# The down projection of three quarters by seven products, for two panels at a time

## The chip, the cores and the metric

The kernel runs on one core of a Trainium2 chip. The metric is the device time of one execution in microseconds, the median of several runs; lower is better.

## The reference, cut to what matters

One step of one layer of a hybrid decoder for 512 prompt tokens and 8 sample tokens, which share all weights. Attention and gated linear attention give `mix`; the change lies in what follows it:

```
def merge_and_ffn(x, ..., w_o, g_norm2, w_up, w_down):
    ...
    h = x + mix @ w_o
    f = jnp.square(jax.nn.relu(rmsnorm(h, g_norm2) @ w_up))      # w_up (1024, 4096)
    return h + f @ w_down                                        # w_down (4096, 1024)
y_prompt, y_sample = rmsnorm(xp, g_final), rmsnorm(xs, g_final)
```

## The kernel before, in words

**Layout.** Activations lie transposed: 128 rows of the model dimension on the partitions, 8 tiles of them (k), 520 columns (512 prompt tokens and 8 sample tokens). `HC` is half of the columns, 260; `halves` shows a tile as two such halves. D = 1024, KT = 8.

**Precision.** Each matrix product is made of three products of fp32r numbers: high part by high part, high by low, low by high (`passes`). A weight is loaded as a panel (128 output columns, 8 k-tiles, 512 KB) by SP's queue, and split in pieces of 4 k-tiles (512 wide): ScalarE copies the high part (`whi`, L128), VectorE subtracts it from the panel for the low part (`wlo`, L131). Activations are split likewise: `hh`, `hl` for the normalized residual H, `fh`, `fl` for the squared relu.

**Direct panels.** `panel_mm` makes one panel with 2 halves x 8 k x 3 = 48 products of 260 columns (L301).

**Pairs by seven products.** `pair_mm` (L229) makes two panels at once with the Strassen-Winograd scheme: the rows of the activations are halved (k 0 to 3, and 4 to 7), the columns too, and of the two panels' weights. Seven products P1 to P7 of 4 k x 3 = 84 matmuls replace 96. They need sums of weights and of activations. Activation sums: `Th`, `Tl` (high and low parts) hold for each k of the first half the four sums of the two rows k and k + 4 and the two column halves; `column_sums` makes them on VectorE as H is made. Weight sums: the loaded panel `sums` is completed by an accumulating DMA on POOL's queue (`load_sums`, L115, up to 28 us ahead); two VectorE adds make two more (`pair_sums`, tile `s`, 512 wide each). P1, P6, P7, P4 accumulate one behind the other in the PSUM bank x, P5 and P3 in e, P2 in a, where P1's result was copied. The order on TensorE is P1, P5, P6, P3, P7, P2, P4. What is done with a result comes as `then(name, a, e, x)` after that product, and "T0", "T1" at the start of the next pair. `lead(i + 1, ...)` splits the next panel's pieces on the way (0: `pair_sums`; 1: P1's piece; 2: P6's with P3's, 1024 wide, and P5's; 3: P7's).

**The order of work.** In the feed-forward part ScalarE and VectorE run strictly in the order of the program: `act`, `add` and `stt` (L128, L131, L134) pass each instruction to `turn`, which chains it behind the last one of its engine. TensorE is chained too (`behind`). `pace` issues copies of the caches (DRAM to DRAM, on POOL's queue).

**Stages.** W_o makes H panel by panel. Then four quarters (qd) of 1024 columns of w_up: 8 panels as four pairs (`up_pair`), each squared relu split into fh, fl, then 8 down panels of w_down's rows for this quarter, added up in `dd`. Up pairs take neighbouring panels i and i + 1. In quarters 0 to 2 the 8 down panels are direct; quarter 0 copies to dd and squares H for the norm into `acc`; quarter 1 spreads the column sum with a matmul by ones (`spread`, rv = 1 / (mean square + eps)); quarter 2 multiplies dd by rv and adds H. In quarter 3 rv is applied to f, and the down panels are made in a last loop (L1500) in column parts of 280 and 240, with the final norm and the output behind them. In an up pair of quarters 0 to 2, f is the first panel's tile and t the second's; the names `P` of the tiles in the trace are PSUM results of P5 and P6 that ScalarE keeps in SBUF (the `keep` in `up_pair`).

## Time and profile before

| | |
|---|---|
| median of 3 runs | 890.13 us (889.88 to 890.97) |
| profiled execution | 890.22 us |
| its span, first to last instruction | 888.3 us |
| mean granted clock of TensorE | 0.997 |
| TensorE busy | 876.6 us, 7962 matmuls |
| VectorE busy | 605.0 us, 1187 instructions |
| ScalarE busy | 428.0 us, 874 instructions |
| memory | 153.31 MB read, 54.17 MB written |

The span is what the trace covers; the execution's own time is 1.9 us longer. Busy times are sums over the instructions of an engine; engines work beside each other. Rows of the timeline read: start in us from the span's start, duration, engine, line, operation, out<-in, shape, and in brackets the idle time ahead of it with the engine that ended it. The products of a panel or pair are a row of matmuls without a gap where the next one is always ready.

### The profile page before, as it was taken

The numbers are of one execution on the slowest core, as the hardware profiler recorded it, in microseconds if no ns is written. First come the engines' busy times: TensorE is split into PE (matmuls) and PEld (weight loads), VectorE is DVE, ScalarE is ACT, GpSimd is POOL, SyncE is SP. The second block draws the span as 40 slices with busy tenths as digits, with TensorE's granted clock in tenths as the row PEclk, the third lists the DMA queues.
The fourth block names the chain that finished last, engine by engine and source line by source line (L and its number), as shares of the span: only waits on it lengthen the run. The fifth ranks groups of instructions, "written<-read, shape, count | busy, mean of one in ns | idle before, by whom it ended". The sixth has DMA issues, their size and how long they took to land.

```text
span 888.3 us, 19424 instructions
## 1 busy us (share of the span) xinstructions
PE 876.6 (99%) x7962; PEld 859.1 (97%) x7962; DVE 605.0 (68%) x1187; ACT 428.0 (48%) x874; POOL 92.6 (10%) x143
## 2 busy tenths in 40 slices
PE   9999999999999999999999999999999999999996
PEld 9999999999999999999999999999999999999995
DVE  6877566775957949695755778636864585579843
ACT  7233424452635536454633557623752375248732
POOL 1110000001111302101000200011101110110000
PEclk9999999999999999999999999999999999999998
DMA  7476465324445443125798875579748775974302
GB/s 258 134 262 215 130 214 200 110 74 149 159 163 186 158 160 140 57 97 191 251 365 296 301 217 167 190 217 281 232 172 261 240 235 184 282 241 148 143 24 74
DMA packets 44385, 168.29 MB, mean 189 GB/s; under 512 B 5821, under 2 KB 10949, under 8 KB 42473
## 3 DMA queue, kind: packets, MB, share of 16 engines
q1 hardware_dynamic: 34552, 98.98, 32.1%
q0 software_dynamic: 9456, 67.59, 23.7%
q8 instruction: 62, 1.02, 0.4%
q10 hardware_dynamic: 288, 0.49, 0.2%
q14 instruction: 27, 0.21, 0.1%
HBM read 153.31 MB, written 54.17 MB: 234 GB/s over the span
## 4 chain that ended last, share of the span: by engine, by line
PE 97%; DVE 1%; DMA 1%; ACT 0%; issue 0%; SPq 0%; DVEq 0%; ACTq 0%
PE mps L301 64%; PE mps L229 17%; PE mps L1500 5%; PE lev L896 1%; PE mps L467 1%; PE sps L642 1%; PE pvp L675 1%; PE gpo L1005 1%; PE gpu L1009 1%; PE ptp L659 1%; PE vps L606 1%; PE gpo L1007 1%; DMA xr<-in_xT 1%; PE gso L1077 0%; PE gop L1029 0%; PE gsp L1094 0%
## 5 line engine op out<-in xcount | busy, mean ns | idle before, releaser
L128 ACT ACTIVATE whi<-raw 128x512 fp32r<-128x512 f32 (+1 forms) x234 | 143.7, 621 | 260.9 <-PE mps L301 225.4
L301 PE MATMUL mps<-uh,whi 128*128 128x260 f32 x896 | 255.8, 286 | 0.0
L301 PE MATMUL mps<-ul,whi 128*128 128x260 f32 x896 | 255.7, 285 | 0.0
L301 PE MATMUL mps<-uh,wlo 128*128 128x260 f32 x896 | 255.2, 285 | 0.0
L131 DVE TENSOR_TENSOR wlo<-raw,whi 128x512 fp32r<-128x512 f32 (+1 forms) x234 | 156.2, 678 | 45.6 <-ACT whi L128 43.3
L301 PEld LDWEIGHTS mps<-uh,wlo 128*128 128x128 f32 x896 | 168.7, 188 | 2.1 <-issue 1.5
L301 PEld LDWEIGHTS mps<-ul,whi 128*128 128x128 f32 x896 | 168.6, 188 | 1.2 <-issue 0.3
L301 PEld LDWEIGHTS mps<-uh,whi 128*128 128x128 f32 x896 | 168.7, 188 | 1.1 <-issue 0.7
L301 PE MATMUL mps<-fh,wlo 128*128 128x260 f32 x384 | 108.5, 283 | 0.0
L301 PE MATMUL mps<-fh,whi 128*128 128x260 f32 x384 | 108.4, 282 | 0.0
L301 PE MATMUL mps<-fl,whi 128*128 128x260 f32 x384 | 108.1, 282 | 0.0
L229 PE MATMUL mps<-Th,whi 128*128 128x260 f32 x256 | 72.5, 283 | 0.4 <-DVE t L131 0.4
L229 PE MATMUL mps<-Tl,whi 128*128 128x260 f32 x256 | 72.3, 282 | 0.1
L301 PEld LDWEIGHTS mps<-fh,whi 128*128 128x128 f32 x384 | 72.3, 188 | 0.0
L301 PEld LDWEIGHTS mps<-fh,wlo 128*128 128x128 f32 x384 | 72.2, 188 | 0.0
L229 PE MATMUL mps<-Th,wlo 128*128 128x260 f32 x256 | 72.2, 282 | 0.0
L301 PEld LDWEIGHTS mps<-fl,whi 128*128 128x128 f32 x384 | 72.2, 188 | 0.0
L229 PE MATMUL mps<-hl,whi 128*128 128x260 f32 x192 | 54.2, 282 | 0.0
L229 PE MATMUL mps<-hh,wlo 128*128 128x260 f32 x192 | 54.2, 282 | 0.0
L229 PE MATMUL mps<-hh,whi 128*128 128x260 f32 x192 | 54.1, 282 | 0.0
L229 PEld LDWEIGHTS mps<-Th,whi 128*128 128x128 f32 x256 | 48.2, 188 | 0.6 <-DVE t L131 0.6
L229 PEld LDWEIGHTS mps<-Tl,whi 128*128 128x128 f32 x256 | 48.1, 188 | 0.3 <-DVE Tl L131 0.3
(370 smaller groups left out, 1838.2 us busy)
## 6 DMA issues: line engine op xcount, KB each, us to landing
raw<-in_w_in SPq DMA_DIRECT2D x55, 512.0 KB, 4.4
raw<-in_w_down SPq DMA_DIRECT2D x32, 512.0 KB, 4.1
sums<-in_w_up SPq DMA_DIRECT2D x16, 512.0 KB, 4.2
sums<-in_w_up POOLq DMA_DIRECT2D x16, 512.0 KB, 8.0
raw<-in_w_up SPq DMA_DIRECT2D x16, 512.0 KB, 5.8
sx<-in_state SPq DMA_DIRECT2D x8, 512.0 KB, 4.4
sx<-dV SPq DMA_DIRECT2D x8, 512.0 KB, 4.8
out_sgla<-sx POOLq DMA_DIRECT2D x8, 512.0 KB, 5.0
```

Of the source, the lines that this page charges most:

```text
L128: return self.turn("ACT", self.nc.scalar.activation(*args, **kw))
L131: return self.turn("DVE", self.nc.vector.tensor_tensor(out, a, b, op=op))
L229: mm = nc.tensor.matmul(o, w[:, k], u, start=(n in ("P1", "P5") and k == 0 and y == 0), stop=(k == 3 and y == 2), skip_group_check=True)
L301: mm = self.nc.tensor.matmul(o[:, :HC], wt, x[:, k, j * HC:(j + 1) * HC], start=(k == 0 and n == 0), stop=(k == kt - 1 and n == 2))
L467: self.last = nc.tensor.matmul(ps[i][:, j, :HC], wt, u[:, k, j * HC:(j + 1) * HC], start=(k == 0 and n == 0), stop=(k == KT - 1 and n == 1))
L606: nc.tensor.transpose(pt[:, r * P:(r + 1) * P], vt[:, r * P:(r + 1) * P], self.c["ident"])
L642: m = nc.tensor.matmul(pss[hh][:, hp, c], Q[rows, i, b * P:(b + 1) * P], K[rows, i, ks], start=True, stop=True)
L659: nc.tensor.transpose(pt[:, hh, x], prs[hp][:, hh, x * P:(x + 1) * P], self.c["ident"])
L675: m = nc.tensor.matmul(po[64 * hh:64 * hh + 64, hp * P:(hp + 1) * P], v, pTs[hp][:, hh, x], start=(x == first), stop=(x == 1))
L896: m = self.nc.tensor.matmul(out, w, x, start=True, stop=True)
L1005: nc.tensor.matmul(po[:, :256], ST[:, c], V[:, c], start=True, stop=(c == 0))
L1500: nc.tensor.matmul(ps, w, u[:, kk, cc], start=(kk == 0 and x == 0), stop=(kk == KT - 1 and x == 2))
```

## The change

It makes the down projection of quarters 0 to 2 in pairs of panels, through `pair_mm` as the up projection is. For that:

- An up pair is now made of panels i and i + 4 of the quarter, so that it gives the rows k and k + 4 of f together, of which `sums`, `high` and `low` in `up_pair` make the four column sums of squared tiles. Sum 0 is written where the second half of hh, hl for the first four k was (that half is no longer written), sums 1 and 2 in a new tile `FT`, sum 3 in the second half of fh, fl for the first four k. The square of f moves from VectorE to ScalarE. The last up pair of a quarter (`end`) has an order of its own.
- `down_pair` adds each product's result to dd (`put`) when it is there: P5's, P6's, P7's, P3's, P2's and P4's. In quarter 0 the first put to each part of dd is a copy on ScalarE.
- `extras`: H is written to the DRAM tile `Hd` in the W_o stage (POOL's queue); quarter 0 loads it back to square it (SP's queue), quarter 2 adds it to dd by an accumulating DMA (POOL's queue). The reciprocal of quarter 1 is made in four parts of 130 columns.
- In `pair_mm` P7's piece of a pair behind a direct panel, and the weight sums of the next pair, are made after P5; a hook "T2" stands there too. The last loop takes k in the order 0, 1, 2, 4, 5, 6, 3, 7, and cache copies that were issued ahead of it are issued within it.

The diff, cut:

```diff
 def pair_mm(self, acts, then):
-        if not first and self.panels[i - 1][1] != PAIR:
-            self.pair_piece(i, "P7")
         if before:
             before("T0")
...
             if n == "P1":
                 if before:
                     before("T1")
-                if first:
+            elif n == "P5":
+                if before:
+                    before("T2")
+                if "P7" not in self.ready[i]:
                     self.pair_piece(i, "P7")
-                elif pair:
-                    self.lead(i + 1, 0)
-            elif n == "P5":
                 self.pair_piece(i, "P4" if first else "P2")
-                if first:
+                if pair:
                     self.lead(i + 1, 0)
...
-            if n == "P2" and pair:
+            if n == "P2" and pair and not then(n + " ends"):
                 self.lead(i + 1, 3)

 def up_pair(self, p, work, k, fh, fl, T, copies, rv):
-        end, short = k == KT - 2, rv is not None and k == KT - 2
+        end, short = k == 3, k == 3 and rv is not None
+        def sums(*steps):
+            f, t = v["f"], v["t"]
+            if "c" not in v:
+                v["c"] = p.tile([P, 3, HC], F32, tag="tr", name="tr", bufs=2)
+            c = v["c"]
+            for n in steps:
+                if n == 1:
+                    self.add(c[:, 0], t[:, two], f[:, two], op=ALU.subtract)
+                elif n == 0:
+                    self.add(f[:, two], f[:, one], f[:, two], op=ALU.subtract)
+                elif n == 2:
+                    self.stt(c[:, 1], c[:, 0], -1.0, f[:, one], op0=ALU.mult, op1=ALU.subtract)
+                else:
+                    self.stt(c[:, 2], c[:, 1], -1.0, t[:, one], op0=ALU.mult, op1=ALU.subtract)
+        def place(n):
+            return (v["f"][:, two], v["c"][:, 0:2], v["c"][:, 2])[n], *T(n, k)
+        def high(n):
+            c, hi, lo = place(n)
+            self.act(hi, c, AF.Copy)
+        def low(n):
+            c, hi, lo = place(n)
+            self.add(lo, c, hi.bitcast(F32), op=ALU.subtract)
...
             elif n == "P7":
-                v["t"] = work()
-                self.add(v["t"][:, two], x, v["P5"])
+                f, t = v["f"], v["t"] = work(), work()
+                self.add(t[:, two], x, v["P5"])
...
+                self.add(f[:, two], e, v["P6"])
+            elif n == "P7 later":
+                f, t = v["f"], v["t"]
+                if not short:
+                    self.act(t[:, two], t[:, two], AF.Relu, scale=-1.0)
+                self.act(f[:, two], f[:, two], AF.Relu)
+                if T and end:
+                    self.act(t[:, two], t[:, two], AF.Square)
+            elif n == "P2":
+                f = v["f"]
+                self.act(f[:, one], a, AF.Relu)
+                self.act(f, f, AF.Square)
...
+                if T and end:
+                    split(0, f, one)
+                    sums(1, 0)
...
             elif n == "T0":
+                f, t = v["f"], v["t"]
+                self.act(t[:, one], x, AF.Relu, scale=-1.0)
+                if T and end:
+                    high(0)
+                    self.act(t[:, one], t[:, one], AF.Square)
+                    low(0)
+                    sums(2, 3)
+                elif T:
                     self.act(t, t, AF.Square)
+                    split(0, f, one)
+                    sums(1, 0, 2, 3)
...
+            elif n == "T1":
+                if T and end:
+                    high(1)
+                    low(1)
+                    self.act(fh[:, k + 4], v["t"], AF.Copy)
+                else:
+                    split(4, v["t"])
+                    if T:
+                        high(0)
+            elif n == "T2" and T:
+                if end:
+                    high(2)
+                    self.add(fl[:, k + 4], v["t"], fh[:, k + 4].bitcast(F32), op=ALU.subtract)
+                    low(2)
+                else:
+                    high(1)
+                    high(2)
+                    for n in range(3):
+                        low(n)
+
+def down_pair(self, k, dd, qd, also):
+        def put(x, cc, o, sign=1):
+            d = dd[:, k + x, cc]
+            if qd == 0 and (x, cc) not in put.begun:
+                put.begun.add((x, cc))
+                self.act(d, o, AF.Copy, scale=float(sign))
+            elif sign < 0:
+                self.add(d, d, o, op=ALU.subtract)
+            else:
+                self.add(d, o, d)
+        put.begun = set()
+        def then(n, a=None, e=None, x=None):
+            if n == "P1":
+                self.act(a, x, AF.Copy)
+            elif n == "P5":
+                put(1, two, e, -1)
+            elif n == "P6":
+                put(0, two, x)
+            elif n == "P7":
+                put(1, two, x, -1)
+                put(0, two, e)
+            elif n == "P2":
+                put(0, one, a)
+            elif n == "P4":
+                self.pace(1)
+            elif n == "T0":
+                put(1, one, x, -1)
+            also(n)
+        return then

 def run(self):
         for qd in range(4):
-            order += [(I["w_up"][qd * 8 + i:qd * 8 + i + 2], PAIR) for i in range(0, 8, 2)]
-            order += [(I["w_down"][i][:, qd * 8:qd * 8 + 8], KT) for i in range(8)]
+            order += [(I["w_up"][qd * 8 + i:qd * 8 + i + 5:4], PAIR) for i in range(4)]
+            ks = slice(qd * 8, qd * 8 + 8)
+            if qd < 3:
+                order += [(I["w_down"][i:i + 2, :, ks], PAIR) for i in range(0, 8, 2)]
+            else:
+                order += [(I["w_down"][i][:, ks], KT) for i in range(8)]
...
+                nc.gpsimd.dma_start(Hd[:, k], H[:, k])
...
+            def T(n, k):
+                return ((hh[:, k, HC:], hl[:, k, HC:]), (FT[:, k, 0:2], FT[:, k, 2:4]), (fh[:, k, HC:], fl[:, k, HC:]))[n]
+            def extras(qd, k):
+                v = {}
+                def also(n):
+                    if qd == 0:
+                        if n == "P1":
+                            for x in range(2):
+                                v[x] = acc if k + x == 0 else work()
+                                self.load(v[x], Hd[:, k + x])
+                        elif n == "P4":
+                            for x in range(2):
+                                self.act(v[x], v[x], AF.Square)
+                                if k + x:
+                                    self.add(acc, acc, v[x])
+                    elif qd == 1:
+                        if n == "P1" and k == 0:
...
+                            self.turn("DVE", nc.vector.tensor_scalar(halves(rv), pr[:, :, :HC], 1 / D, EPS,
+                                                                     op0=ALU.mult, op1=ALU.add))
+                        elif n == "P4":
+                            c = slice(65 * k, 65 * k + 130)
+                            self.turn("DVE", nc.vector.reciprocal(rv[:, c], rv[:, c]))
+                    elif n in ("P4", "T0"):
+                        x = k + (n == "T0")
+                        self.add(dd[:, x], dd[:, x], rv, op=ALU.mult)
+                        nc.gpsimd.dma_start(dd[:, x], Hd[:, x], accum_op=ALU.add)
+                return also
...
-                for k in range(KT):
-                    ps = self.panel_mm(fh, fl)
-                    dv = halves(dd[:, k])
-                    if qd == 0:
-                        self.turn("DVE", nc.vector.tensor_copy(dv, ps))
-                        sq = work() if k else acc
-                        self.act(sq, H[:, k], AF.Square)
-                        if k:
-                            self.add(acc, acc, sq)
-                    else:
-                        self.add(dv, ps, dv)
-                    if qd == 2:
-                        self.add(dd[:, k], dd[:, k], rv, op=ALU.mult)
-                        self.add(dd[:, k], dd[:, k], H[:, k])
-                    if qd == 1 and k == 0:
-                        spread()
-                    self.pace(k % 2)
-            self.pace(1000)
+                for k in range(0, KT, 2):
+                    self.pair_mm(down_acts, self.down_pair(k, dd, qd, extras(qd, k)))
...
-                    for kk in range(KT):
+                    for kk in (0, 1, 2, 4, 5, 6, 3, 7):
...
+                    if j == 0 and k > 2:
+                        self.pace(1 if k < KT - 2 else 1000)

```

VectorE in a middle up pair of the third quarter (qd 2), from its first add on a result in PSUM (`t<-mps,P`): before, where the first row adds P3's result (f) and the third P7's (t), and the weight pieces are the next pair's,

```order
L131 TENSOR_TENSOR t<-mps,P_9369 128x260
L131 TENSOR_TENSOR wlo<-raw,whi 128x512
L131 TENSOR_TENSOR t<-mps,P_9351 128x260
L131 TENSOR_TENSOR wlo<-s,whi 128x1024
L131 TENSOR_TENSOR wlo<-sums,whi 128x512
L134 SCALAR_TENSOR_TENSOR t<-t 128x520
L131 TENSOR_TENSOR wlo<-sums,whi 128x512
L131 TENSOR_TENSOR fl<-t,fh 128x520 x2
L131 TENSOR_TENSOR s<-sums,raw 128x512
L131 TENSOR_TENSOR s<-s,raw 128x512
L131 TENSOR_TENSOR wlo<-raw,whi 128x512
L131 TENSOR_TENSOR wlo<-rb,whi 128x512
```

and now, where both adds wait for P7 and stand in the first two rows (t, then f), `tr`, `FT` and `hl` belong to the column sums, and the last low part is that of sum 3:

```order
L131 TENSOR_TENSOR t<-mps,P_9532 128x260
L131 TENSOR_TENSOR t<-mps,P_9558 128x260
L131 TENSOR_TENSOR wlo<-s,whi 128x1024
L131 TENSOR_TENSOR wlo<-sums,whi 128x512 x2
L131 TENSOR_TENSOR fl<-t,fh 128x260
L131 TENSOR_TENSOR tr<-t 128x260
L131 TENSOR_TENSOR t<-t 128x260
L134 SCALAR_TENSOR_TENSOR tr<-tr,t 128x260 x2
L131 TENSOR_TENSOR fl<-t,fh 128x520
L131 TENSOR_TENSOR hl<-t,hh 128x260
L131 TENSOR_TENSOR FT<-tr,FT 128x520
L131 TENSOR_TENSOR fl<-tr,fh 128x260
```

A 520-wide square (`t<-t`, L134) is gone; four column sums (`tr<-tr,t` twice, `tr<-t`, `t<-t`) and three low parts have come, and `s` stands further on, behind them.

ScalarE at the same place, from the high part of P5's piece: before, where the relu of t's second half, the relu of f's first half, P7's weight copy, and the relu and square of t follow it,

```order
L128 ACTIVATE whi<-sums 128x512
L128 ACTIVATE t<-t 128x260
L128 ACTIVATE t<-mps 128x260
L128 ACTIVATE whi<-sums 128x512
L128 ACTIVATE t<-mps 128x260
L128 ACTIVATE t<-t 128x520
L128 ACTIVATE fh<-t 128x520
L128 ACTIVATE mps<-mps 128x260
L128 ACTIVATE fh<-t 128x520
```

and now:

```order
L128 ACTIVATE whi<-sums 128x512
L128 ACTIVATE t<-t 128x260 x2
L128 ACTIVATE t<-mps 128x260
L128 ACTIVATE t<-t 128x520
L128 ACTIVATE whi<-sums 128x512
L128 ACTIVATE t<-mps 128x260
L128 ACTIVATE t<-t 128x520
L128 ACTIVATE fh<-t 128x260
L128 ACTIVATE mps<-mps 128x260
L128 ACTIVATE fh<-t 128x520
L128 ACTIVATE hh<-t 128x260
```

The relu of f's second half and the square of f (520 wide) now stand on ScalarE between the relu of t and the weight copy for P7's piece; the copies of the column sums begin at the end.

VectorE at the start of the third quarter's down stage, where the low parts of the last squared tile are made: before, with the panel's add, rv and H for each panel,

```order
L131 TENSOR_TENSOR wlo<-raw,whi 128x512
L134 SCALAR_TENSOR_TENSOR t<-t 128x520
L131 TENSOR_TENSOR fl<-t,fh 128x520 x2
L131 TENSOR_TENSOR wlo<-raw,whi 128x512 x2
L131 TENSOR_TENSOR dd<-mps,dd 128x520
L131 TENSOR_TENSOR dd<-dd,rv 128x520
L131 TENSOR_TENSOR dd<-dd,H 128x520
L131 TENSOR_TENSOR wlo<-raw,whi 128x512 x2
L131 TENSOR_TENSOR dd<-mps,dd 128x520
L131 TENSOR_TENSOR dd<-dd,rv 128x520
L131 TENSOR_TENSOR dd<-dd,H 128x520
```

and now:

```order
L134 SCALAR_TENSOR_TENSOR tr<-tr,t 128x260 x2
L131 TENSOR_TENSOR FT<-tr,FT 128x520
L131 TENSOR_TENSOR dd<-dd,mps 128x260
L131 TENSOR_TENSOR fl<-t,fh 128x520
L131 TENSOR_TENSOR fl<-tr,fh 128x260
L131 TENSOR_TENSOR wlo<-sums,whi 128x512
L131 TENSOR_TENSOR wlo<-raw,whi 128x512
L131 TENSOR_TENSOR s<-sums,raw 128x512
L131 TENSOR_TENSOR s<-s,raw 128x512
L131 TENSOR_TENSOR dd<-mps,dd 128x260
L131 TENSOR_TENSOR wlo<-rb,whi 128x512
L131 TENSOR_TENSOR wlo<-raw,whi 128x512
L131 TENSOR_TENSOR dd<-dd,mps 128x260
```

Of the puts, `dd<-dd,mps` on the third row is P5's, `dd<-mps,dd` P6's, which stands behind two low parts of weights and the two sums `s`.

96 lines of the change are left out of this document (42 added, 54 removed).

## Prediction

> **What bounds the kernel now.** I read the page's busy shares and its chain first, then busy time by stage, then the order in time of VectorE and ScalarE inside one pair.
>
> ```profile
> span 888.3 us, 19424 instructions
> PE 876.6 (99%) x7962; PEld 859.1 (97%) x7962; DVE 605.0 (68%) x1187; ACT 428.0 (48%) x874; POOL 92.6 (10%) x143
> PE 97%; DVE 1%; DMA 1%; ACT 0%; issue 0%; SPq 0%; DVEq 0%; ACTq 0%
> ...
> 655.50:701.40 45.90, 45.90 (x386) 45.90 (x385) 22.16 (x32) 13.41 (x24) 5.77 (x7) 1.00 0.81 264
> 701.50:741.60 40.10, 40.10 (x338) 40.10 (x338) 30.57 (x49) 26.78 (x54) 3.30 (x5) 1.00 0.59 198
> ...
> L301 PE MATMUL mps<-fh,wlo 128*128 128x260 f32 x384 | 108.5, 283 | 0.0
> ```
>
> TensorE (PE) is busy 99% and holds 97% of the chain. The two window rows are the direct down stage of one quarter and the up stage of the next (after the length: PE, weight load, DVE, ACT, POOL busy, clock, DMA share, GB/s). TensorE has no gap in either. VectorE (DVE) is busy 22.2 of 45.9 us in the down stage, but 30.6 of 40.1 in the up stage by pairs, and the change puts work into both. The last row: 24 down panels hold 384 products of each of three kinds, 16 x 3 = 48 a panel.
>
> **The saving.** A panel's end shows when VectorE reads it:
>
> ```profile
> 686.22 0.70 DVE L131 TENSOR_TENSOR dd<-mps,dd 128x520 f32<-128x520 f32 x1 [3.84 <-PE mps L301]
> 691.96 0.70 DVE L131 TENSOR_TENSOR dd<-mps,dd 128x520 f32<-128x520 f32 x1 [3.84 <-PE mps L301]
> ...
> 706.31 0.39 ACT L128 ACTIVATE P<-mps 128x260 f32<-128x260 f32 x1 [1.07 <-PE mps L229]
> 716.35 0.39 ACT L128 ACTIVATE P<-mps 128x260 f32<-128x260 f32 x1 [0.46 <-PE mps L229]
> ```
>
> 5.74 us a panel is 0.1196 us a product; a pair (7 x 4 x 3 = 84 products) takes 10.04. Two panels cost 11.48, so each of the 12 new pairs saves 12 products or 1.44 us: **17.2 us**, if TensorE stays fed. The Trainium skill, "TensorE: Matmul & The Clock Gate", section "Wait — 56ns, not 53.3ns?", gives a warm product its column count over 2.4 GHz plus about 2.5 ns. As an estimate from that page 260 columns take 0.111 us and the saving is 16.0; the trace differs with its 0.1196, and the trace decides.
>
> **What the up pairs pay.** In an up pair of quarters 0 to 2 VectorE gains the four differences of column sums and the low parts of three tiles, and loses one 520-wide square, which goes to ScalarE (ACT). The prices are distances from start to start in one run of each engine:
>
> ```profile
> 710.61 0.43 DVE L131 TENSOR_TENSOR t<-mps,P 128x260 f32<-128x260 f32 x1 [0.30 <-PE mps L229]
> 710.96 1.22 DVE L131 TENSOR_TENSOR wlo<-s,whi 128x1024 fp32r<-128x1024 f32 x1
> 712.09 0.68 DVE L131 TENSOR_TENSOR wlo<-sums,whi 128x512 fp32r<-128x512 f32 x1
> 712.69 0.69 DVE L134 SCALAR_TENSOR_TENSOR t<-t 128x520 f32<-128x520 f32 x1
> 713.30 0.68 DVE L131 TENSOR_TENSOR wlo<-sums,whi 128x512 fp32r<-128x512 f32 x1
> 715.09 1.53 DVE L131 TENSOR_TENSOR fl<-t,fh 128x520 fp32r<-128x520 f32 x2 [1.11 <-ACT fh L128]
> 716.54 0.68 DVE L131 TENSOR_TENSOR s<-sums,raw 128x512 f32<-128x512 f32 x1
> 717.26 0.69 DVE L131 TENSOR_TENSOR s<-s,raw 128x512 f32<-128x512 f32 x1
> 717.87 0.69 DVE L131 TENSOR_TENSOR wlo<-raw,whi 128x512 fp32r<-128x512 f32 x1
> ...
> 831.70 0.43 DVE L134 SCALAR_TENSOR_TENSOR t<-mps,rv 128x260 f32<-128x260 f32 x1 [0.93 <-PE mps L229]
> 832.16 0.43 DVE L134 SCALAR_TENSOR_TENSOR t<-mps,t 128x260 f32<-128x260 f32 x1
> ...
> 711.07 0.42 ACT L128 ACTIVATE t<-t 128x260 f32<-128x260 f32 x1
> 712.05 0.39 ACT L128 ACTIVATE t<-mps 128x260 f32<-128x260 f32 x1 [0.56 <-PE mps L229]
> 713.47 0.39 ACT L128 ACTIVATE t<-mps 128x260 f32<-128x260 f32 x1 [0.51 <-PE mps L229]
> 713.89 0.64 ACT L128 ACTIVATE t<-t 128x520 f32<-128x520 f32 x1
> 714.44 0.62 ACT L128 ACTIVATE fh<-t 128x520 fp32r<-128x520 f32 x1
> 714.96 0.37 ACT L128 ACTIVATE mps<-mps 128x260 f32<-128x260 f32 x1
> 715.27 0.62 ACT L128 ACTIVATE fh<-t 128x520 fp32r<-128x520 f32 x1
> ...
> 711.85 0.28 PE L229 MATMUL mps<-Th,whi 128*128 128x260 f32 x1
> 538.74 0.39 PE L229 MATMUL mps<-Th,whi 128*128 128x260 f32 x1 [0.39 <-DVE t L131]
> 538.97 0.28 PE L229 MATMUL mps<-Tl,whi 128*128 128x260 f32 x1
> ```
>
> VectorE steps: 260 wide 0.35, 512 0.60, 520 0.61, 1024 1.13; 0.46 (260) or 0.72 (512) if the next reads what it wrote. ScalarE: 260 wide 0.31, 512 0.52, 520 0.55, and 0.42 from a relu to the square that reads it. From a ScalarE end to the VectorE read 0.03 (714.44 + 0.62 to 715.09); from the next product's start to the read of the last one 0.20 (711.85 to 712.05).
>
> Follow a middle up pair from X, its first low part (fl, 260). VectorE's list up to the second PSUM add f is six steps of 0.35, two of 0.46, two 520 (1.22), three 512 (1.80), and the two sums s (0.72 + 0.60): f starts at X + 7.37. Then ScalarE: relu of f's half when f is done (+0.46), next relu +0.31, square +0.42, P7's weight copy +0.55, T0's relu +0.52, square +0.42, high copy +0.55, its own 0.42 and 0.03: the next X is f + 3.68. One round is 11.05 us against TensorE's 10.04. VectorE itself has only about 10.0 us of work in it; it waits some 1.0 us for that ScalarE chain. So each middle pair comes **1.0 us** later than TensorE needs. At first this is covered by weights split ahead.
>
> Quarter's first pair is on time (VectorE has slack behind a down pair): its chain starts when P2 can be read, 7.17 + 1.44 + 0.20 = 8.81, and X of the second pair is 2.91 later, 11.72, or 1.68 into that pair. X is then 2.69 and 3.70 into the third and fourth, and f of the fourth at F = 11.07.
>
> **What the first down pair pays.** Its product P7 accumulates on the bank that P6 left, so it waits until P6's result is added to dd. In quarters 1 and 2 that add stands on VectorE behind low parts and two weight sums. From F: two relus, square, relu, square of f (0.11, 0.46, 0.77, 1.08, 1.50), high copy at 2.17, fl 2.62, two sums 2.97 and 3.43, high copy of T0 3.89, its low part 4.34, sums 4.69 and 5.15, copy of FT, then VectorE without a gap: FT 5.80, P5's put 6.41, fl 6.76 and 7.37, P7 7.72, P2 8.32, s 8.92 and 9.64, P6's put 10.25. It lasts 0.43; TensorE restarts 0.06 behind (538.26 + 0.42, the add of the row below, to 538.74) and loses 0.11 on its first product (0.23 instead of 0.12): 10.85. P7 starts at 11.07 + 10.85 = 21.9, on time would be 10.04 + 5.74 = 15.8: **6.1 us** in quarter 2, earlier waits of TensorE included. In quarter 1 the rv step adds 0.3 and the ones products, part of the time now, take off 0.7: **5.7**.
>
> ```profile
> 538.26 0.42 DVE L131 TENSOR_TENSOR t<-mps,P 128x260 f32<-128x260 f32 x1
> 649.27 1.04 PE L1442 MATMUL r<-acc,ones 128*128 128x260 f32 x4
> 649.96 0.47 PE L229 MATMUL mps<-Th,whi 128*128 128x260 f32 x1
> ...
> 538.47 0.61 ACT L128 ACTIVATE whi<-sums 128x512 fp32r<-128x512 f32 x1
> 540.47 0.39 ACT L128 ACTIVATE t<-mps 128x260 f32<-128x260 f32 x1 [0.29 <-PE mps L229]
> ```
>
> In quarter 0 ScalarE makes the first two puts: P7 at F + 8.44, but the first up pair follows W_o late. Its relus can come only behind the copy at 538.47, so X is 542.5, 0.55 later than 540.27 + 1.68: loss **4.3**. The other down pairs are nearly even: P5's put 3.07, P2 3.42, s 4.02 and 4.74, P6's put 5.35 to 5.78 with 0.17 behind it, against 5.74: 0.2 in each of six, **1.3**.
>
> Losses 17.4; with 0.34 for a 260-wide step they are 16.6. I take 17.0. Both ends: no loss if these queues ran ahead; twice the loss if each step were late by as much again.
>
> **What costs nothing.** VectorE in a down pair: weights 3.0 + 1.13 + 1.33, puts 6 x 0.35, 7.6 of 10.04; quarter 2's two products with rv add 1.2, quarter 1's reciprocals 0.7 to 0.9. The put that subtracts from PSUM, and the negated copy, are not in this trace; nearest are the 0.43 and 0.39 above, ends 0.3 and 0.7, six a pair beside TensorE's products. The residual in DRAM: eight writes and eight accumulating adds on POOL's queue, eight loads on SP's. What is behind them on POOL are the accumulates into the weight sums:
>
> ```profile
> DMA to landing us min/median/max: 5.6/8.0/12.8
> ```
>
> They are issued some 13 us before VectorE reads them, so the median is hidden and the maximum just; the adds into dd wait on VectorE for about 2 us of that. If that cover goes, s is late, then P6's put. The squares read loads issued a pair earlier; late ones would hold ScalarE's queue. Five cache copies move from quarter 3's up stage and behind it into the last stage, off the chain. The order of k there and the changed place of P7's piece keep all products. The add of H falls away on VectorE, under TensorE's time.
>
> **Sum.** 890.22 (span 888.3 and 1.9 around it) - 17.2 + 17.0 = 890.0; the profiled run lies 0.1 above the median 890.13. The measurement tells about 0.2% (1.8 us) from no change.
>
> **Rivals.** *The queues catch up* (faster). If no round is late, F is 9.05: 4.1 + 3.7 + 1.7 + 1.3 = 10.8 lost, 883.8; if P6's put is in time too, 874.3. For it: VectorE's own work fits into 10.04. Against: strict order on both engines. It decides if f is followed by less than 2.7 us of ScalarE.
>
> *The clock falls in the waits* (slower).
>
> ```profile
> 879.00:880.00 1.00, 0.70 (x4) 0.52 (x4) 0.00 (x0) 0.40 (x3) 0.00 (x0) 1.00 0.00 0
> 882.00:883.00 1.00, 0.00 (x0) 0.00 (x0) 0.96 (x3) 0.00 (x0) 0.00 (x0) 1.00 0.00 0
> 883.00:884.00 1.00, 0.00 (x0) 0.00 (x0) 1.00 (x3) 0.00 (x0) 0.00 (x0) 0.68 0.36 123
> ```
>
> After the last product (879.9) the clock holds until about 883.4, 3.5 us. The wait before P7 is 2.3 us (P3 ends at F + 8.4). Were it over 3.5, by 1.2 us more lateness in each of three quarters (3.6), and the clock at half for as long again (1.7 each, 5.2), the time is 890 + 9 = 899; halves of it give 894. Against: every stage at 1.00 so far. The Trainium skill, same page, section "What's actually happening", halves the clock after an idle window of about 3.4 us; the trace agrees with its 3.5.
>
> **How the numbers follow.** No measurable change by the sum (888.3 to 891.9): 0.42. Queues catch up, wholly or in part (874 to 888.3): 0.36. Clock, late sums or longer queues (892 to 900): 0.22. The range 882 to 896 leaves out a tenth at each side; the likeliest case alone is 888 to 892. So faster 0.36, same 0.42, slower 0.22.
>
> **What would show it.** Right: up windows of about 41 to 42 us with TensorE gaps ended by VectorE or ScalarE; one gap of about 2 us in P7 of the first down pair in quarters 1 and 2, ended by a dd add on VectorE; down pairs 10.0 to 10.3. Wrong: quarters of 80.3 us with no gap (the saving whole), or gaps ended by DMA of the sums, or a clock below 1.00.

## The result

The changed kernel takes 898.75 us (median of 4 runs, 895.87 to 899.72) against 890.01 us before: slower, ratio 1.009 (95% interval 1.0066 to 1.0114). The profiled run took 898.83 us, its span is 897.1. The forecast was 890.0, with 882 to 896.

From the page of the changed kernel, the span, the busy shares and the engines of the chain that ended last:

```profile
span 897.1 us, 19539 instructions
PE 870.5 (97%) x7818; PEld 847.2 (94%) x7818; DVE 659.1 (73%) x1333; ACT 473.3 (53%) x989; POOL 118.8 (13%) x171
...
PE 84%; DMA 5%; DVE 5%; ACT 3%; issue 1%; SPq 0%; DVEq 0%; ACTq 0%; POOLq 0%
```

144 products are gone, as they should be (7962 to 7818), but the chain, 97% TensorE before, is now 84%. The view of waits says for TensorE (line, engine and line waited for, us in total, times, longest us):

```profile
PE mps L227 <- ACT whi L128: 9.8, 13, 3.0
PE mps L227 <- DVE dd L131: 4.4, 2, 2.2
```

The table gives each stage from the start of its first product to that of the next stage (us; quarter 3's up stage ends with the last product of its last pair, and the last column runs to the span's end). "Forecast" is, from the prediction, the saving, the first down pair's loss and, in quarters 1 and 2, the 0.2 of each later down pair, against the kernel before. These columns sum to +0.2; the prediction took 17.0 for losses that sum to 17.4, so its span is -0.2.

| | entry | quarter 0 | quarter 1 | quarter 2 | quarter 3, up | rest | span |
|---|---|---|---|---|---|---|---|
| before | 529.25 | 87.04 | 86.94 | 86.06 | 42.21 | 56.80 | 888.3 |
| changed | 530.28 | 85.84 | 87.17 | 89.01 | 47.31 | 57.49 | 897.1 |
| difference | +1.0 | -1.2 | +0.2 | +3.0 | +5.1 | +0.7 | +8.8 |
| forecast | 0 | -1.4 | +0.6 | +1.0 | 0 | 0 | -0.2 |

Quarters 0 and 1 came within 0.4 us of the forecast. Quarter 2 lost 2 us more, and quarter 3's up stage, in which the forecast had no term, lost 5.

**The up pairs.** VectorE in a middle pair of quarter 2, from one add on P7's result to the next, and TensorE's product P4 of two pairs (start, duration, in brackets the idle time and what ended it):

```profile
722.63 0.76 DVE L131 TENSOR_TENSOR t<-mps,P 128x260 f32<-128x260 f32 x2
...
725.34 0.69 DVE L131 TENSOR_TENSOR wlo<-sums,whi 128x512 fp32r<-128x512 f32 x1 [0.22 <-ACT whi L128]
726.59 0.43 DVE L131 TENSOR_TENSOR fl<-t,fh 128x260 fp32r<-128x260 f32 x1 [0.56 <-ACT fh L128]
...
733.58 0.75 DVE L131 TENSOR_TENSOR t<-mps,P 128x260 f32<-128x260 f32 x2
...
723.20 0.36 PE L227 MATMUL mps<-Th,whi 128*128 128x260 f32 x1 [0.66 <-ACT whi L128]
734.14 0.36 PE L227 MATMUL mps<-Th,whi 128*128 128x260 f32 x1 [0.66 <-ACT whi L128]
```

A round is 10.95 us, with 0.78 in which VectorE waits for ScalarE. TensorE stands before P4, since P4 accumulates on the bank from which VectorE must first add P7's result; P4's own weight copy, which began at 719.13, was long done. So the releaser that the rows name, a ScalarE copy that happens to end then, is not the cause: in the program P4 waits for the add and for its own weights.

**The first down pair of quarters 1 and 2**, TensorE at P7, and in quarter 2 VectorE ahead of it:

```profile
668.18 0.48 PE L227 MATMUL mps<-FT,whi 128*128 128x260 f32 x2 [2.22 <-DVE dd L131]
755.67 0.49 PE L227 MATMUL mps<-FT,whi 128*128 128x260 f32 x2 [2.20 <-DVE dd L131]
...
751.29 0.42 DVE L131 TENSOR_TENSOR dd<-dd,mps 128x260 f32<-128x260 f32 x1
...
753.17 0.69 DVE L131 TENSOR_TENSOR wlo<-raw,whi 128x512 fp32r<-128x512 f32 x1
753.77 0.69 DVE L131 TENSOR_TENSOR s<-sums,raw 128x512 f32<-128x512 f32 x1
754.49 0.69 DVE L131 TENSOR_TENSOR s<-s,raw 128x512 f32<-128x512 f32 x1
755.10 0.42 DVE L131 TENSOR_TENSOR dd<-mps,dd 128x260 f32<-128x260 f32 x1
```

The add of P6's result stands behind the weight sums without a gap, and TensorE restarts 0.57 after it began: the wait that the forecast worked out as 2.3 us.

**The clock after such waits** (columns as in the prediction's window rows; the clock is the last but two):

```profile
755.60:759.80 4.20, 4.13 (x22) 4.16 (x23) 2.88 (x5) 1.37 (x2) 0.00 (x0) 0.60 0.60 178
824.90:828.20 3.30, 3.27 (x15) 3.30 (x16) 3.16 (x5) 2.40 (x7) 0.03 (x1) 0.51 0.02 6
668.20:672.20 4.00, 4.00 (x33) 4.00 (x34) 3.33 (x6) 1.92 (x3) 0.00 (x0) 1.00 0.61 199
```

After the wait of 2.20 us at 755.67 the clock fell; after that of 2.22 at 668.18 it did not. P7 to the next pair's P1 takes 5.93 us in quarter 2 and 4.39 in quarter 1, so it cost 1.5.

**Quarter 3's up stage.** TensorE at P4 of its first and third pair, VectorE at the weight sums for the fourth, their load (SP's queue) and accumulating transfer (POOL's queue), and a window row of the time that the load took, with the DMA engines' share in the last but one column (a packet counts whole in the window in which it starts, so the share can exceed 1):

```profile
801.61 0.36 PE L227 MATMUL mps<-Th,whi 128*128 128x260 f32 x1 [0.52 <-ACT whi L128]
824.93 0.56 PE L227 MATMUL mps<-Th,whi 128*128 128x260 f32 x1 [3.00 <-ACT whi L128]
821.82 0.69 DVE L131 TENSOR_TENSOR s<-sums,raw 128x512 f32<-128x512 f32 x1 [3.97 <-DMA sums<-in_w_up]
800.97 0.43 SPq L87 DMA_DIRECT2D sums<-in_w_up  x1
813.03 1.21 POOL L115 DMA_DIRECT2D sums<-in_w_up  x1 [8.92 <-ACT t L128]
800.97:813.03 12.06, 11.54 (x96) 11.45 (x96) 11.43 (x20) 10.85 (x24) 0.53 (x1) 1.00 1.15 336
```

and in the kernel before the same load, accumulate and sum, with such a row:

```profile
795.83 0.42 SPq L87 DMA_DIRECT2D sums<-in_w_up  x1
800.40 1.27 POOL L115 DMA_DIRECT2D sums<-in_w_up  x1
812.72 0.69 DVE L131 TENSOR_TENSOR s<-sums,raw 128x512 f32<-128x512 f32 x1
795.83:800.40 4.57, 4.57 (x40) 4.57 (x39) 3.99 (x6) 4.40 (x9) 0.49 (x1) 1.00 0.74 279
```

The load went out at 800.97 and the accumulate could start only when it had landed, 12.1 us later (4.6 before); that took another 8.8 (8.1 before). VectorE stood 3.97 us before `s`, behind `s` stands the add on P7's result, and P4 waited 3.00. The DMA engines' share was 1.15 while the load was under way, where it had been 0.74. Over the whole stage it was 0.87 against 0.51, and at 271 and 171 GB/s the stage moved 12.8 MB, against 7.2.

### The profile page after: what moved, and what is told of

Read it like the earlier page. It is cut to its first block, busy times and chain, and to the rows that moved or that the text cites. A ratio compares the mean times of both kernels' runs of the same rounds, so it can differ in the third digit from the quotient of the medians.

```text
span 897.1 us, 19539 instructions
## 1 busy us (share of the span) xinstructions
PE 870.5 (97%) x7818; PEld 847.2 (94%) x7818; DVE 659.1 (73%) x1333; ACT 473.3 (53%) x989; POOL 118.8 (13%) x171
## 3 DMA queue, kind: packets, MB, share of 16 engines
HBM read 167.01 MB, written 56.30 MB: 249 GB/s over the span
## 4 chain that ended last, share of the span: by engine, by line
PE 84%; DMA 5%; DVE 5%; ACT 3%; issue 1%; SPq 0%; DVEq 0%; ACTq 0%; POOLq 0%
PE mps L299 48%; PE mps L227 21%; PE mps L1612 5%; DMA sums<-in_w_up 4%; ACT t L128 1%; PE lev L894 1%; PE mps L465 1%; ACT whi L128 1%; PE sps L640 1%; DVE s L131 1%; DVE fl L131 1%; PE pvp L673 1%; DVE wlo L131 1%; PE gpo L1003 1%; PE gpu L1007 1%
## 5 line engine op out<-in xcount | busy, mean ns | idle before, releaser
L128 ACT ACTIVATE whi<-raw 128x512 fp32r<-128x512 f32 (+1 forms) x210 | 128.8, 619 | 180.4 <-PE mps L299 146.7
L131 DVE TENSOR_TENSOR wlo<-raw,whi 128x512 fp32r<-128x512 f32 (+1 forms) x210 | 141.5, 677 | 58.7 <-ACT whi L128 57.5
L227 PE MATMUL mps<-hl,whi 128*128 128x260 f32 x240 | 68.1, 284 | 0.0
L227 PE MATMUL mps<-hh,whi 128*128 128x260 f32 x240 | 68.1, 284 | 0.0
L227 PEld LDWEIGHTS mps<-Th,whi 128*128 128x128 f32 x256 | 48.7, 190 | 12.1 <-ACT whi L128 11.3
L227 PE MATMUL mps<-fh,whi 128*128 128x260 f32 x192 | 54.9, 286 | 0.3 <-ACT whi L128 0.3
L227 PE MATMUL mps<-fl,whi 128*128 128x260 f32 x192 | 54.8, 286 | 0.0
L227 PE MATMUL mps<-fh,wlo 128*128 128x260 f32 x192 | 54.5, 284 | 0.0
L128 ACT ACTIVATE whi<-s 128x1024 fp32r<-128x1024 f32 x28 | 29.7, 1060 | 40.2 <-DVE s L131 25.4
L227 PEld LDWEIGHTS mps<-Th,wlo 128*128 128x128 f32 x256 | 48.8, 191 | 0.0
L1612 PE MATMUL mps<-fh,lw 128*128 128x280 f32 (+1 forms) x256 | 47.3, 285 | 0.4 <-ACT fh L128 0.4
```

Source lines behind the costliest of these rows:

```text
L128: return self.turn("ACT", self.nc.scalar.activation(*args, **kw))
L131: return self.turn("DVE", self.nc.vector.tensor_tensor(out, a, b, op=op))
L227: mm = nc.tensor.matmul(o, w[:, k], u, start=(n in ("P1", "P5") and k == 0 and y == 0), stop=(k == 3 and y == 2), skip_group_check=True)
L1612: self.last = nc.tensor.matmul(ps, w, u[:, kk, cc], start=(kk == 0 and x == 0), stop=(kk == KT - 1 and x == 2))
```

## The experiments

All medians are of runs beside runs of the kernel before on the same chip (890.05 to 890.71). Stages are those of one profiled run of each, as in the table above, and need not be those of the median run: e6's profiled run (889.36) is its fastest, e7's (893.46) one of its slowest (888.21 to 894.37).

| run | median | ratio (95%) | entry | q0 | q1 | q2 | q3 up | rest |
|---|---|---|---|---|---|---|---|---|
| e1_put_first | 898.78 | 1.0081 to 1.0111 | 530.1 | 90.2 | 85.9 | 87.8 | 45.6 | 57.4 |
| e2_sums_lead | 899.84 | 1.0093 to 1.0137 | 529.0 | 93.0 | 89.1 | 86.9 | 41.8 | 56.7 |
| e3_lows_later | 896.75 | 1.0053 to 1.0083 | 530.1 | 85.2 | 87.7 | 85.8 | 49.2 | 57.3 |
| e4_no_residual_add | 895.00 | 1.0038 to 1.0067 | 530.0 | 85.9 | 88.8 | 88.4 | 42.6 | 57.1 |
| e5_copies_early | 898.70 | 1.0068 to 1.0112 | 534.2 | 88.5 | 87.2 | 88.7 | 41.8 | 57.9 |
| e6_order_copies | 891.65 | 1.0002 to 1.0021 | 531.4 | 85.6 | 85.4 | 85.6 | 41.8 | 57.8 |
| e7_order_lead | 889.40 | 0.9987 to 1.0020 | 529.8 | 91.7 | 85.4 | 85.6 | 41.8 | 57.4 |
| e8_all | 893.90 | 1.0028 to 1.0062 | 533.1 | 87.5 | 85.4 | 85.6 | 41.8 | 57.8 |
| e9_lead_later | 898.34 | 1.0080 to 1.0111 | 530.1 | 87.8 | 89.1 | 88.4 | 41.8 | 57.4 |
| e10_best | 885.21 | 0.9934 to 0.9959 | 530.1 | 84.8 | 85.0 | 85.2 | 41.9 | 57.1 |
| e11_best_old_lead | 890.27 | 0.9994 to 1.0017 | 529.0 | 84.8 | 85.0 | 85.7 | 47.0 | 56.7 |

**e1_put_first: the add of P6's result ahead of weight work**

```diff
 elif n == "P5":
-    pair_piece(i, "P7"); pair_piece(i, "P2"); lead(i + 1, 0)   # first down pair of a quarter
 elif n == "P6":                                                # behind the add of P6's result
+    pair_piece(i, "P7", "P2")
     pair_piece(i, "P4")
+    lead(i + 1, 0)
```

> Only the first down pair of each quarter is changed: P7's and P2's weight pieces and the next pair's weight sums come behind the add of P6's result into dd, not ahead of it. Theory A (P7 waits because that add stands in VectorE's strict queue behind four weight steps): the add comes about 2.5 us earlier (four steps of 0.60 to 0.72), the waits of 2.2 us ahead of P7 in quarters 1 and 2 vanish, and so does the stretch of half clock that follows the one in quarter 2 (1.6 us); the time falls by 4.5 to 6 us, to about 893. Theory B (the late column sums and weight copies would hold the next product anyway): the wait moves to P7's weight piece or to P4, and the time falls by less than 1.5 us.

The waits of 2.2 us are gone, and with them every stretch of half clock. What is left in that pair is a wait ahead of P4, for the add of P7's result, which now stands behind the weight sums:

```profile
673.97 0.36 PE L227 MATMUL mps<-fh,whi 128*128 128x260 f32 x1 [0.66 <-DVE dd L131]
...
618.81 0.36 PE L227 MATMUL mps<-fh,whi 128*128 128x260 f32 x1 [3.08 <-ACT whi L128]
813.88 0.36 PE L227 MATMUL mps<-Th,whi 128*128 128x260 f32 x1 [1.09 <-ACT whi L128]
826.31 0.36 PE L227 MATMUL mps<-Th,whi 128*128 128x260 f32 x1 [2.15 <-ACT whi L128]
```

Theory A names the wait's cause, and quarters 1 and 2 are 1.3 and 1.2 us shorter. The time did not fall: the weight sums were late at more places (3.08 at the end of quarter 0, 1.15 in quarter 2, 1.09 and 2.15 in quarter 3), 7.5 us where the changed kernel lost 3.5. e1 was not ahead of the changed kernel at these places; at the end of quarter 0 the load ahead of the accumulate took 12.9 us there against 7.2. Why these transfers were slower in e1 is not shown.

**e2_sums_lead and e9_lead_later: weight sums asked for three pairs ahead**

```diff
-LEAD = 28.0
+LEAD = 38.0                                                             # e2
-if self.at[j] - self.at[i] > LEAD:
+if self.at[j] - self.at[i] > LEAD + 10 * (i > self.first_pair + 1):     # e9, from the third up pair on
```

> The weight sums are asked for three pairs ahead instead of two (the limit of 28 us becomes 38); the three buffers stay. Theory A (in quarter 3 the load of the summed panel is issued too late, because it stands on SP's queue behind the load of another half panel that waits for VectorE): the load goes out about 7 us earlier, the waits of 0.5 and 3.0 us in quarter 3 vanish with the half clock behind the second (1.5 us), and the time falls by about 5 us, to 893 to 894. Theory B (the transfers themselves are slow there, 8 to 12 us each, since too much is moved at a time): issuing earlier only lengthens them, and the time falls by less than 1.5 us.

> One edit: the weight sums are asked for three pairs ahead from the third up pair on, and as in the change before it, so that the entry from W_o is left alone. Theory A (in quarter 3 the sums come late because their load is asked for too late, and nothing else is wrong with the lead): the up stage of quarter 3 falls from 47.3 to about 41.9 us, the entry stays at 530 us, and the time falls by 4 to 5 us, to 894. Theory B (the earlier loads push other transfers back): the loads of H in quarter 0, which stand behind them on SP's queue, come later and hold ScalarE's squares there; the down stage of quarter 0 grows by 2 to 7 us, and the time falls by less than 2 us.

In both, quarter 3's up stage takes 41.8 us, without any wait: there theory A holds, although the DMA engines were as full (a share of 0.87 over the stage in both; e2: 1.03 to 1.08 from 780 to 820). Both medians stay where they were, and the price shows. In e2 the fourth pair's load found no free buffer, and SP's queue stood still behind it:

```profile
507.92 0.42 SPq L87 DMA_DIRECT2D rb<-in_w_up  x1
535.22 0.33 SPq L87 DMA_DIRECT2D sums<-in_w_up  x1
535.60 0.42 SPq L87 DMA_DIRECT2D raw<-in_w_up  x1
...
542.80 0.58 PE L227 MATMUL mps<-Th,whi 128*128 128x260 f32 x1 [4.73 <-DVE t L131]
```

The second pair's own panel (`raw`) came 27 us after the load ahead of it in the queue, and TensorE waited 4.73 us. In e9 this is gone (entry 530.1, no such wait), but the loads of H for the norm in quarter 0 now stand behind the sums, and ScalarE waits for them in its strict order:

```profile
598.62 1.31 ACT L128 ACTIVATE t<-t 128x520 f32<-128x520 f32 x2 [3.06 <-DMA t<-Hd]
...
600.54 0.51 PE L227 MATMUL mps<-FT,whi 128*128 128x260 f32 x2 [1.62 <-ACT mps L128]
```

Quarter 0's down stage grew by 1.9 us, just under the 2 to 7 of theory B, which is right for e9's total: 0.4 us gained on the median of the changed kernel. Part of the rest is half clock, which followed both waits ahead of P7 in e9's profile, and one of the two in the changed kernel's.

**e3_lows_later: the same work in VectorE's idle time**

```diff
 # "T2" of an up pair
-for n in range(3): low(n)
+low(0); self.lows = low
 # "P2" of the next up pair, where VectorE waited for ScalarE
+self.lows(1); self.lows(2)
```

> In the up pairs of quarters 0 to 2 the low parts of the last two column-sum tiles (0.61 and 0.35 us on VectorE) are made one pair later, in the place where VectorE now waits 0.22 and 0.56 us for ScalarE. The work is the same. Theory A (each of these rounds lasts 10.95 us because VectorE waits for ScalarE's chain of relu, square and copy inside it): the waits are filled, a round falls to 10.2 us, the waits of 0.66 us ahead of P4 fall below 0.2, about 0.8 us in each of nine rounds, and the time falls by 5 to 7 us, to about 892 to 894. Theory B (VectorE's work itself, or the weights' buffers, set the round): the rounds stay at 10.8 to 11, and the time within 1.5 us.

```profile
742.66 0.36 PE L227 MATMUL mps<-Th,whi 128*128 128x260 f32 x1 [0.20 <-ACT whi L128]
...
728.47 0.69 DVE L131 TENSOR_TENSOR wlo<-raw,whi 128x512 fp32r<-128x512 f32 x1 [0.37 <-ACT whi L128]
...
822.39 0.56 PE L227 MATMUL mps<-Th,whi 128*128 128x260 f32 x1 [4.26 <-ACT whi L128]
```

A round falls to 10.48 us (adds on P7's result at 721.14 and 731.62), the wait ahead of P4 from 0.66 to 0.20. Half of the idle time moved to another place (0.37). The up stages of quarters 0 to 2 are 1.4 to 2.1 us shorter each, and the late sums of quarter 3 take it back: 4.26 us and half clock behind it. Theory A for the rounds, though 10.2 was expected; the time fell by 2.0 only.

**e4_no_residual_add: what the residual's transfers cost**

```diff
 self.add(dd[:, x], dd[:, x], rv, op=ALU.mult)
-nc.gpsimd.dma_start(dd[:, x], Hd[:, x], accum_op=ALU.add)
```

> The eight accumulating transfers that add the residual to dd in quarter 2 are left out, so the output lacks the residual; it is still written to memory and read back for the norm. Theory A (the load order sets the late weight sums of quarter 3): the waits there stay, and the time changes by less than 1 us. Theory B (these transfers, of 11.8 us median to landing, hold the accumulates of the weight sums on POOL's queue or take their bandwidth): the waits of 0.5 and 3.0 us in quarter 3 and the half clock behind them go, and the time falls by 4 to 5 us, to 894.

The wait of 3.0 us becomes 0.51 (822.42), the half clock behind it goes, quarter 3's up stage falls to 42.6. The last pair's load took as long (issued 800.15, accumulate at 812.62), but the accumulate landed in 6.7 us, not 8.8. Counted from the start of the stage the sums came 3.3 us earlier, 2.1 by this and 1.2 by an earlier issue. So theory B: the time fell by 3.8 us, and most of it is bandwidth rather than POOL's queue, in which the accumulate waits for its own load in both. Together with e2 and e5: the sums were late by a lead of two pairs and full DMA engines together; a longer lead (e2) or fewer copies (e5) alone removes all waits in this stage.

**e5_copies_early: bandwidth from cache copies**

```diff
-self.proj_scaled(gA)
-self.proj_scaled(gB, 4)
+self.proj_scaled(gA, 0)      # a cache copy behind each of the 16 panels
+self.proj_scaled(gB, 0)
```

> Twelve of the cache copies (1 MB read and 1 MB written each) are issued twelve panels earlier, in the projections of the gates, where the DMA engines are 0.2 to 0.5 busy; quarters 2 and 3 and the last stage then have none left. Queues, load order and VectorE's work in the feed-forward part stay. Theory A (the late weight sums of quarter 3 are a matter of bandwidth: the DMA engines are 0.9 to 1.2 busy from 770 to 820 us): the loads and accumulates there land in 4 to 7 us instead of 9 to 12, the waits of 0.5 and 3.0 us and the half clock behind them go, and the time falls by 4 to 5 us, to about 894. Theory B (the order of issue alone): they stay, and the time changes by less than 1.5 us.

Quarter 3's up stage is 41.8 without a wait, as theory A says (DMA share 0.67 over the stage, 181 GB/s instead of 271). The time did not fall, for the copies delay the attention stages: TensorE waits there that the changed kernel does not have,

```profile
PE mps L299 <- DVE gA L1133: 2.4, 1, 2.4
PE gsp L1092 <- ACT ov L1087: 1.2, 1, 1.2
```

and the first up pair starts at 534.2 instead of 530.3. Weight sums were late at the end of quarter 0 too, as in e1 (a wait of 2.43 us at 621.19). The stretch with a low average share had loads in it that are waited for: from 330 to 480 us ScalarE waits 10.3 us for panels of `in_w_in`, where it waited 4.5.

**e6, e7, e8: the edits together**

In these, the first down pair's weight sums stand behind the add of P7's result, so that P4 does not wait for it either.

```diff
 elif n == "P7":                       # first down pair: behind the add of P7's result
+    lead(i + 1, 0)                    # e1 had this behind P6's
     lead(i + 1, 2)
 # e6: with e3 and e5;  e7: with e3 and e9;  e8: with e3, e5 and e9
```

> Three edits at once: the early copies; the low parts one pair later; and in each quarter's first down pair the add of P6's result ahead of the weight pieces, with the weight sums behind the add of P7's result, so that P4 does not wait for that add either. If the three losses are separate (late weight sums 5 us, rounds of the up pairs 3 to 4 us, the wait ahead of P7 2.4 us in each of two quarters, with half clock 1.6), they add up: 898.8 - 12 = 886 to 888, below the 890 of the kernel before. If the limit is one and the same (VectorE's queue hands each gain on to the next wait), the time stays above 892.

> As the run with three edits, but with the copies where the change has them, and instead the weight sums asked for three pairs ahead from the third up pair on (not in the W_o stage, where this delayed the first pairs). If issuing earlier does as much as freeing bandwidth, 886 to 888 too; if bandwidth is what lacks, waits for the weight sums show up at other places and it stays at 890 or above.

> All four edits: early copies, sums three pairs ahead, low parts later, the first down pair's order. What is left are rounds of 10.47 us in the up pairs (0.43 lost in each of nine), 0.2 in each down pair, and some entry losses of 1 us: 17.2 - 3.9 - 2.4 - 3 = 8 us below the kernel before, 882 to 885.

All three have the same 85.4 and 85.6 in quarters 1 and 2 and 41.8 in quarter 3's up stage: these losses can be removed together. What differs is what pays for the weight sums. With early copies the entry is 1 to 3 us late; with the longer lead the loads of H are late (e7: waits of 1.30 and 2.92 us in quarter 0, then half clock, 91.7). e8 has both prices and is the slowest of the three, against my sum (882 to 885). e6 is slower than before by about 0.1%, e7 can't be told from it; for both the first expectation, 886 to 888, was missed.

**e10_best: H squared where it is made**

```diff
 # W_o stage, behind the low part of each panel of H (the last one in the first up pair)
+self.act(t, H[:, k], AF.Square)
+if k: self.add(acc, acc, t)
 # quarter 0's down pairs
-self.load(v[x], Hd[:, k + x]); self.act(v[x], v[x], AF.Square); self.add(acc, acc, v[x])
 # first down pair, behind P7's result: P5's weight piece does not wait for the weight sums
+self.pair_piece(i + 1, "P5"); self.lead(i + 1, 0); self.pair_piece(i + 1, "P6")
 # last up pair of a quarter: self.lows(2) at "P2", self.lows(1) at "T0";  with e3's low parts, e6's order and e9's lead
```

> The lead from the third pair on; the low parts of two sums later; in the first down pair the adds ahead of the weight sums, with P5's weight piece of the next pair ahead of them too; and H squared for the norm in the W_o stage from SBUF, so that quarter 0 loads nothing back. If each loss has the cause that the runs so far gave it: quarter 0 lasts 85, quarters 1 and 2 84 us each, quarter 3's up stage 41.8, with waits of 0.2 us ahead of P4 and none above 0.7; the sum against the kernel before is 2 + 3 + 2 = 7 us less: 882 to 885. If the squares in the W_o stage hold the entry, or waits come back elsewhere: 887 to 890.

885.21 us (884.92 to 885.99), ratio 0.9946 (0.9934 to 0.9959): faster than both, by 4.8 us than before and by 13.5 than the change. TensorE's waits in the feed-forward part (compare the two rows at the head):

```profile
PE mps L227 <- DVE dd L131: 2.7, 4, 1.1
PE mps L227 <- DVE t L131: 0.6, 1, 0.6
PE mps L227 <- ACT whi L128: 0.4, 2, 0.3
```

None reaches 1.2 us, there is no half clock in the stage, and the runs lie within 1.1 us, where the changed kernel's lay within 3.9. The median lies 0.2 us above the expected 882 to 885. Quarters 1 and 2 are 1.0 and 1.2 us longer than expected: the second down pair now waits for the adds into dd ahead of P3 and P7 (0.54 and 0.54 us in quarter 1, 1.05 and 0.55 in quarter 2), which are the four waits of the first row.

**e11_best_old_lead: the lead alone, on the best kernel**

```diff
-if self.at[j] - self.at[i] > LEAD + 10 * (i > self.first_pair + 1):
+if self.at[j] - self.at[i] > LEAD:
```

> The best kernel so far with the weight sums asked for two pairs ahead again, as in the change. Theory A (the lead is what the up stage of quarter 3 needs, and asking earlier cost something only where H was loaded back): quarter 3's up stage grows from 41.9 to 46 to 49 us with waits for the weight sums, the rest stays, and the time rises by 4 to 7 us, to 889 to 892. Theory B (without the loads of H and with the shorter queues on VectorE the sums are in time anyway): the time stays at 885 to 886.

Theory A: quarter 3's up stage is 47.0 instead of 41.9, with waits of 1.05 and 1.98 us and half clock behind the second; the other stages agree within 0.6, and the entry is 1.1 earlier. The median rises by 5.1, to 890.27.

```profile
804.38 0.36 PE L227 MATMUL mps<-Th,whi 128*128 128x260 f32 x1 [1.05 <-ACT whi L128]
816.67 0.36 PE L227 MATMUL mps<-Th,whi 128*128 128x260 f32 x1 [1.98 <-ACT whi L128]
```

## Why the prediction was wrong

- **The step that failed** is "They are issued some 13 us before VectorE reads them, so the median is hidden and the maximum just". The accumulate's own time was right: 8.8 us for the late one, in the prediction's 5.6 to 12.8. But it was issued 8.8 us ahead, not 13, because the load that it waits for took 12.1 us instead of 4.6. The prediction took its 13 us from the kernel before, where only the last sums of an up stage were asked for so late, and the DMA engines' share was 0.74 while they were loaded, not 1.15. How long ahead of the `s` that reads them (us) load and accumulate were issued, for the four pairs of quarter 3:

| | pair 1 | pair 2 | pair 3 | pair 4 |
|---|---|---|---|---|
| before: load, accumulate | 32.7, 26.5 | 34.0, 25.3 | 31.8, 21.8 | 16.9, 12.3 |
| changed: load, accumulate | 17.7, 10.7 | 19.9, 9.0 | 18.9, 13.3 | 20.9, 8.8 |

In the changed kernel `s` waited 1.49 us for pair 2's sums and 3.97 for pair 4's. In the prediction no term priced the added bytes (153.31 to 167.01 MB read, 54.17 to 56.30 written), and "Five cache copies move from quarter 3's up stage and behind it into the last stage" misread where they lie: three came into the last stage, and quarter 3's up stage has four (795.20, 803.58, 813.80, 828.17) where it had two (789.75, 799.78). With these copies gone from it the stage is on time (e5). The lead is worth 5.1 us by itself (e10 against e11), the same as quarter 3's loss in the result, and "late sums" stood only in a rival, bundled with others at 892 to 900.
- **The clock** was held to need a wait of 3.5 us, with 2.3 forecast and measured. It fell after one of the two waits of 2.2 us: 1.5 us in quarter 2, and again after the wait of 3.00 us in quarter 3. The rival's mechanism was right, its point of decision wrong: the 3.5 us that it read after the last product were one wholly idle window of 3.41 us, and a window idle for 1.90 us was enough (last section).
- **The first down pair** was sized right: 2.20 and 2.22 us ahead of P7, from the order on VectorE that the prediction followed (e1). From the first up product to P7 quarter 2 took 52.4 us against 45.9 on time, 6.5 lost; 6.1 was forecast (quarter 1: 6.2 and 5.7; quarter 0: 4.9 and 4.3).
- **The up pairs' round** was forecast as 11.05 and is 10.95, of which 0.78 is waiting for ScalarE, 1.0 forecast (e3). But no weights split ahead covered it: P4 waited in 10 of the 12 up pairs of quarters 0 to 2, for a bank that VectorE had not yet read. The loss was the same, only paid earlier.
- **The saving** of 12 products a pair came in full, and the down pairs after the first take 10.05 us in quarter 0 and 10.24 in quarters 1 and 2, within the forecast 10.0 to 10.3.
- **Not in the sum**: 1.0 us at the entry and 0.7 at the end. The entry's is there already at 282 us, ahead of all that the change touches, and e10 and e11, which are the same up to the third up pair, start the first one at 530.1 and 529.0; its cause stays open.

```profile
281.15 12.45 PE mps L301 x104
```
```profile
282.11 12.47 PE mps L299 x104
```

(the chain of before, and of the changed kernel, at the same products).

## What to carry to other kernels

When a change makes a stage of transfers continuous that had pauses, durations to landing from the trace of before no longer hold: add up bytes by stage first, with every transfer that changes its place, and compare the lead of each load with load and accumulate at full engines. A wait named in the trace after an engine's copy may hang on another operand; look up what the instruction waits for in the program. And before work is taken away from the bound engine, follow the strict queues that feed it: what was won here came only when adds that free a bank stood ahead of work that can wait, and when nothing that a strict queue waits for was loaded late.

## What the runs showed of the hardware

A wait much shorter than 3.5 us can halve TensorE's clock, and whether it does depends on where the wait falls. In the eleven profiles of the changed kernel, e1 to e5, e7 to e11 (e6 had no wait above 0.9 us), 20 waits in the feed-forward part lasted 1.98 to 4.73 us; half clock followed 13 of them. It began at most 1.5 us behind the restart and lasted 3.4 us (once 6.8, e3). Waits of 2.2 us ahead of P7 did so in 8 of 12. None of 1.80 us or less did. One of 3.08 us did not (e1), one of 1.98 did (e11).

Within each trace all falls of the clock lie whole multiples of 3.41 us apart. Cut at these times, the thirteen profiles have 14 windows up to the last product in which TensorE stood still for 1.90 us or more in all; half clock followed each of them. It followed none at full clock with 1.87 us or less. (One window at half clock with 1.58 us was followed by another, e3.) So the wait of 2.20 us at 755.67 of the changed kernel, whole in one window, halved the clock of the next, and that of 2.22 at 668.18, cut into 1.72 and 0.50, did not; the 3.08 us of e1 were cut into 1.44 and 1.64. The two windows at each of the first two waits, the clock in the last column but two:

```profile
753.02:756.43 3.41, 1.21 (x10) 1.03 (x9) 3.38 (x7) 1.60 (x3) 0.00 (x0) 1.00 0.45 81
756.43:759.84 3.41, 3.41 (x18) 3.41 (x17) 2.09 (x4) 0.63 (x1) 0.00 (x0) 0.50 0.75 225
...
664.27:667.68 3.41, 1.69 (x14) 1.49 (x12) 3.38 (x7) 1.46 (x3) 0.00 (x0) 1.00 0.88 147
667.68:671.10 3.42, 2.92 (x24) 2.95 (x25) 2.75 (x7) 1.70 (x2) 0.00 (x0) 1.00 0.43 116
```

The Trainium skill, "TensorE: Matmul & The Clock Gate", section "What's actually happening", has the clock fall after an idle window of about 3.4 us that runs freely; the steps of 3.41 us agree, but here 1.90 us without a product within one window was enough.
